# Down projection: nine of 22 pairs with seven products, their weight sums made by accumulating DMAs

## The chip, the cores and the metric

The kernel runs on one core of a Trainium2 chip. TensorE (PE) multiplies, VectorE (DVE) and ScalarE (ACT) do the elementwise work, GpSimd (POOL) and SyncE (SP) can issue DMAs, as ACT can. The metric is the device time of one execution in microseconds; the kernel before took 1520.84 us (median of three runs, 1520.27 to 1521.56).

## The reference

One decoder block on 256 tokens of width 2048, with 16 meta tokens in front. After the attention and recurrence halves (left out here) comes the feed-forward part, whose last product is what the change touches:

```python
def _layer(h, ...):
    ...
    h = h + merged @ w_o
    gate, up = jnp.split(_rms(h, n2) @ w_gu, 2, axis=-1)
    return h + (jax.nn.silu(gate) * up) @ w_dn      # (256 x 5632) @ (5632 x 2048)
```

All tensors are float32.

## The kernel before, in words

A float32 product is made of three matmuls: a number is split into a high part (`float32r`, by an ACT copy) and a low part (DVE: the number minus its high part), and high x high, low x high and high x low are added in PSUM. So each weight block passes through: a load from HBM into a `raw` tile (four buffers, issued by SP), the split into `wh` and `wl` (ACT, then DVE; four buffers each, `WB`), and then the matmuls. The function `product` is one such triple of 512-column matmuls (lines 1460 to 1462).

The down projection contracts over 5632 = 22 pairs of blocks of 128 rows. For each of two column groups `cg` of 1024 columns, a pair is a 2 x 2 block product: two row blocks k of the weight by two column blocks x of 512, against two k by two token halves t of the activations `ach`, `acl`. A plain pair (`slow_jobs`) is two jobs with one 512 KB load and four products each, eight products in all; they add into four PSUM tiles `cs` (named `dn`). A fast pair (`fast_jobs`) makes the same with seven products out of sums of weight blocks and sums of activation blocks (a Winograd form of Strassen's scheme): three of them go to `cs`, four to the PSUM tiles `ps` (named `dnp`), which `sums_of_products` adds and takes apart at the end of a column group. Pairs 0 to 6 are fast.

The sums of activations (`sums_of_pairs`, lines 1431, 1444, 1445) are made once, in batches of pairs, when the up projection ends; they are kept in `sst`, which takes the place of the up projection's input `hts` (the same tag in pool `hp`). The sums of weights are made in each column group: `load2` has four DVE subtractions of 128 x 512 (line 1515) between `raw` tiles and two `tt` tiles, which are then split as weights are.

`run(jobs)` sets the order in which the program is written: it emits the load and split of a job, then the matmuls of the job before (`pending`), so that a load is written one job ahead; `finish_job` emits the last pending matmuls. `slot` counts time in the program's own estimate and emits due streams, such as the batches of `sums_of_pairs`, between products. The engines' final order in this stage is made by a planner that places an instruction on its engine when its inputs and buffers are expected to be there, earlier-written ones first; on the chip each engine and each DMA-issuing queue then runs its own list in order. `ORDER` says which pairs follow each other: in the first column group eight plain pairs, then fast and plain ones in turn; in the second, two plain ones around each fast one, and a plain pair at the end. `post` adds the finished tiles to the residual `hh` and stores it (lines 1561, 1562).

Of the kernel before, what the change touches and what calls it, by code (L numbers as in the profile page):

```python
# [18 lines left out]
P = 128  # L19
# [3 lines left out]
T = 256  # L23
# [18 lines left out]
for _n, _k in (("n1", 16), ("mu", 24), ("mu_w", 1), ("mu_a", 1), ("mu_g", 2), ("w0", 8), ("a0", 8), ("k_k", 8),  # L42
# [22 lines left out]
MIX = 0.47  # L65


FAST = [0, 1, 2, 3, 4, 5, 6]
BATCHES = (2, 2, 2, 1)
SLOW = list(range(7, 22))  # L70
ORDER = [SLOW[:8] + [i for pair in zip(FAST, SLOW[8:]) for i in pair],
         [i for n, f in enumerate(FAST) for i in (SLOW[2 * n], f, SLOW[2 * n + 1])] + SLOW[14:]]
PAIRS = 5500

HOP = 3050
SPREAD = 12000
# [40 lines left out]
def hybrid_block(ctx, tc, A, out, dbg=None):  # L117
# [391 lines left out]
    def split(hi, lo_, src):  # L509
        nc.scalar.activation(hi, src, AF.Copy)  # L510
        nc.vector.tensor_tensor(lo_, src, hi.bitcast(F32), op=ALU.subtract)
# [825 lines left out]
    for j in range(4):  # L1337
        js = slice(j * 512, (j + 1) * 512)
        nc.sync.dma_start(hh[:, :, js], x[:, js].rearrange("(t p) c -> p t c", p=P))

        def post(t, ps, j=j, js=js):
            nc.vector.tensor_tensor(hh[:, t, js], ps, hh[:, t, js], op=ALU.add)
            jk = hp.tile([P, 512], F32, tag="jk", name=f"jk{j}{t}", bufs=2)
            nc.scalar.activation(jk, hh[:, t, js], AF.Square, accum_out=ss2[:, t, j:j + 1])
            if t == 0:
                return
            for k in range(4 * j, 4 * j + 4):
                pt = aux_ps(f"hT{k}")[:, :T]
                for t in range(2):
                    nc.tensor.transpose(pt[:, t * P:(t + 1) * P], hh[:, t, k * P:(k + 1) * P], ident)  # L1350
                tmp = hp.tile([P, T], F32, tag="htmp", name=f"htmp{k}", bufs=3)
# [59 lines left out]
    fast = FAST  # L1411
    slow = [i for i in range(NF // 2) if i not in fast]
    acp_h, acp_l = (t.rearrange("p (i k) (t c) -> p i k t c", k=2, t=2) for t in (ach, acl))
    sst = hp.tile([P, KT, 2, L], F32R, tag="hts", name="sst").rearrange("p k a t -> p (k a t)")
    sst = sst[:, :len(fast) * 6 * P].rearrange("p (i s a c) -> p i s a c", i=len(fast), s=3, a=2)

    def sums_of_pairs():

        at = 0
        for n in BATCHES:  # L1420
            fs, ps_ = slice(at, at + n), slice(fast[at], fast[at] + n)
            at += n
            h = lambda k, t: acp_h[:, ps_, k, t, :].bitcast(F32)
            l = lambda k, t: acp_l[:, ps_, k, t, :].bitcast(F32)
            f = [sst[:, fs, i, 1, :] for i in range(3)] + [acp_l[:, ps_, 0, 1, :]]
            hi = [sst[:, fs, i, 0, :] for i in range(3)] + [acp_h[:, ps_, 0, 1, :]]
            f32 = [hp.tile([P, T], F32, tag="ga", name=f"s{at}{i}", bufs=8)[:, :n * P].rearrange("p (i c) -> p i c", c=P)
                   for i in range(4)]

            def tt(i, x_, y_, op):  # L1430
                nc.vector.tensor_tensor(f32[i], x_, y_, op=op)
# [22 lines left out]
    def rows(ap):  # L1454
        return ap.rearrange("p (r c) -> p r c", c=T)

    def product(ps, a, w, half, first, last):
        o = ps.rearrange("p (a c) -> p a c", a=2)
        hi, lo_ = (x_[:, 2 * half:2 * half + 2] for x_ in w)
        nc.tensor.matmul(o, a[0], hi, start=first, stop=False)  # L1460
        nc.tensor.matmul(o, a[1], hi, start=False, stop=False)  # L1461
        nc.tensor.matmul(o, a[0], lo_, start=False, stop=last)  # L1462
        slot(3 * 512 / 2.4)

    def split_tiles():
        return [wp.tile([P, WCOLS], F32R, tag=t, name=t, bufs=WB).rearrange("p (r c) -> p r c", c=L)[:, :, s:s + T]
                for t, s in zip(("wh", "wl"), PLACE_T)]
# [17 lines left out]
            return load, mul  # L1485
        return [mk(0), mk(1)]

    def fast_jobs(i, cg, cs, ps, end):
        box = {}

        def b(k, x_):
            return wdn[i * 256 + k * P:i * 256 + (k + 1) * P, cg * 1024 + x_ * 512:cg * 1024 + (x_ + 1) * 512]

        def load0():
            ra, rb = (wp.tile([P, 1024], F32, tag="raw", name="raw", bufs=RAWB) for _ in range(2))
            nc.sync.dma_start(ra, wdn[i * 256:i * 256 + P, cg * 1024:(cg + 1) * 1024])
            for x_ in range(2):
                nc.sync.dma_start(rb[:, (1 - x_) * 512:(2 - x_) * 512], b(1, x_))
            box["r"] = rows(ra), rows(rb)
            w = split_tiles()  # L1500
            split(*(t[:, 0:2] for t in w), box["r"][0][:, 0:2])
            return w

        def load1():
            w = split_tiles()
            split(*w, box["r"][1])
            return w

        def load2():
            (b11, b12), (b22, b21) = ([r[:, 0:2], r[:, 2:4]] for r in box["r"])  # L1510
            w, v = split_tiles(), split_tiles()
            ts = [rows(hp.tile([P, 1024], F32, tag="tt", name="tt", bufs=2)) for _ in range(2)]
            t1, t2, t3, t4 = (t[:, 2 * n:2 * n + 2] for t in ts for n in range(2))
            for o, x_, y_ in ((t1, b12, b11), (t2, b22, t1), (t3, b22, b12), (t4, b21, t2)):
                nc.vector.tensor_tensor(o, x_, y_, op=ALU.subtract)
            split(*w, ts[0])
            box["v"] = v, ts[1]
            return w

        def load3():  # L1520
            v, t = box["v"]
            split(*v, t)
            return v

        first = i == fast[0]

        def mul0(w):
            if not ps:
                ps.extend(aux_ps(f"dnp{cg}{n}") for n in range(4))
            product(ps[0], a_of(i, 0, 0), w, 0, first, end)  # L1530

        def mul1(w):
            product(cs[1], s_of(i, 3), w, 0, False, False)
            product(cs[0], a_of(i, 1, 0), w, 1, False, False)

        def mul2(w):
            product(ps[1], s_of(i, 0), w, 0, first, end)
            product(ps[2], s_of(i, 1), w, 1, first, end)

        def mul3(w):  # L1540
            product(ps[3], s_of(i, 2), w, 0, first, end)
            product(cs[2], a_of(i, 1, 1), w, 1, False, False)
            if end:
                sums_of_products(cg, ps)
        return [(load0, mul0), (load1, mul1), (load2, mul2), (load3, mul3)]

    def sums_of_products(cg, ps):
        p1, p5, p6, p7 = ps
        h11, h12, h21, h22 = (hh[:, t, (2 * cg + x_) * 512:(2 * cg + x_ + 1) * 512] for t in range(2) for x_ in range(2))
        u = hp.tile([P, 512], F32, tag="jk", name=f"u{cg}", bufs=2)  # L1550
        nc.scalar.activation(u, p1, AF.Copy)
        for o, x_ in ((u, p6), (h11, p1), (h12, p5), (h12, u), (u, p7), (h22, p5), (h21, u), (h22, u)):
            nc.vector.tensor_tensor(o, x_, o, op=ALU.add)

    def post(cg, t, x_, ps):

# [15 lines left out]
    finish_job()  # L1572
    hp_pool.__exit__(None, None, None)
    ap_pool.__exit__(None, None, None)

# [60 lines left out]
```

## Time and profile before

| what | value |
|---|---|
| median of three runs | 1520.84 us |
| lowest and highest run | 1520.27, 1521.56 us |
| profiled execution: its span, first to last instruction | 1517.7 us; no other time is given for it |
| TensorE busy | 1509.9 us of the span |
| down projection in the trace | 1278.3 us to the end |
| DVE / ACT busy between 1278 and 1514 us | 191.2 / 118.9 us |

The trace names instructions by line, engine and the program's tiles (`wh<-raw` is the high part's split). A matmul's row is longer than the distance to the next one, since matmuls overlap. `L510`/`L511` are the lines of the helper `split` (ACT, DVE), `L335`/`L336` those of the same split inside `wload`, which plain jobs use.

### The profile page before, as it was taken

The numbers are of one execution on the slowest core, as the hardware profiler recorded it, in microseconds if no ns is written. First come the engines' busy times: TensorE is split into PE (matmuls) and PEld (weight loads), VectorE is DVE, ScalarE is ACT, GpSimd is POOL, SyncE is SP. The second block draws the span as 40 slices with busy tenths as digits, with TensorE's granted clock in tenths as the row PEclk, the third lists the DMA queues.
The fourth block names the chain that finished last, engine by engine and source line by source line (L and its number), as shares of the span: only waits on it lengthen the run. The fifth ranks groups of instructions, "written<-read, shape, count | busy, mean of one in ns | idle before, by whom it ended". The sixth has DMA issues, their size and how long they took to land.

```text
span 1517.7 us, 26174 instructions
## 1 busy us (share of the span) xinstructions
PE 1509.9 (99%) x10071; PEld 1339.5 (88%) x10071; DVE 1112.0 (73%) x2009; ACT 808.3 (53%) x1230; POOL 99.3 (7%) x182
## 2 busy tenths in 40 slices
PE   9999999999999999999999999999999999999998
PEld 9999999999989888998888888888888888887887
DVE  7888699689789857875665666566566658879776
ACT  7664565475465545644554555454455545554543
POOL 2112202202202000000000000000000000000000
PEclk9999999999999999999999999999999999999999
DMA  8557456646645757777566666666666666566664
GB/s 271 166 166 212 119 156 185 170 122 173 188 127 149 223 152 214 234 231 240 181 179 192 189 187 193 191 186 192 190 187 191 193 186 182 178 211 201 213 206 138
DMA packets 210365, 283.32 MB, mean 187 GB/s; under 512 B 24320, under 2 KB 129296, under 8 KB 210240
## 3 DMA queue, kind: packets, MB, share of 16 engines
q1 hardware_dynamic: 205344, 277.25, 61.9%
q10 hardware_dynamic: 4896, 4.40, 0.9%
q8 instruction: 79, 1.29, 0.3%
q14 instruction: 46, 0.38, 0.1%
HBM read 274.36 MB, written 7.24 MB: 186 GB/s over the span
## 4 chain that ended last, share of the span: by engine, by line
PE 95%; DVE 3%; DMA 1%; issue 1%; ACT 0%; SPq 0%; DVEq 0%; ACTq 0%
PE up L441 11%; PE gt L441 11%; PE zg L441 8%; PE gt L443 5%; PE up L443 5%; PE dn L1461 4%; PE dn L1460 4%; PE dn L1462 4%; PE zg L443 4%; PE f L441 2%; PE br L365 2%; PE br L366 2%; PE br L367 2%; PE f L365 2%; PE wo L1329 2%; PE wo L1331 2%
## 5 line engine op out<-in xcount | busy, mean ns | idle before, releaser
L336 DVE TENSOR_TENSOR wl<-raw,wh 128x1024 fp32r<-128x1024 f32 x460 | 561.9, 1226 | 281.3 <-ACT wh L335 280.6
L335 ACT ACTIVATE wh<-raw 128x1024 fp32r<-128x1024 f32 x460 | 486.5, 1059 | 470.2 <-PE up L441 118.9
L441 PE MATMUL gt<-hts,wh 128*128 128x512 f32 x704 | 242.9, 393 | 0.0
L441 PE MATMUL up<-hts,wh 128*128 128x512 f32 x704 | 242.7, 392 | 0.0
L443 PE MATMUL gt<-hts,wl 128*128 128x256 f32 x660 | 184.8, 280 | 0.0
L443 PE MATMUL up<-hts,wl 128*128 128x256 f32 x660 | 184.6, 280 | 0.0
L441 PE MATMUL zg<-xhl,wh 128*128 128x512 f32 x512 | 181.2, 399 | 0.0
L441 PEld LDWEIGHTS up<-hts,wh 128*128 128x128 f32 x704 | 130.0, 188 | 25.2
L441 PEld LDWEIGHTS gt<-hts,wh 128*128 128x128 f32 x704 | 129.9, 188 | 25.1
L443 PE MATMUL zg<-xhl,wl 128*128 128x256 f32 x480 | 134.3, 280 | 0.0
L443 PEld LDWEIGHTS up<-hts,wl 128*128 128x128 f32 x660 | 125.3, 190 | 1.8
L443 PEld LDWEIGHTS gt<-hts,wl 128*128 128x128 f32 x660 | 125.3, 190 | 1.8
L441 PEld LDWEIGHTS zg<-xhl,wh 128*128 128x128 f32 x512 | 94.3, 188 | 18.7 <-issue 0.7
L1460 PE MATMUL dn<-wh,ach 128*128 128x512 f32 x282 | 110.7, 393 | 0.0
L1461 PE MATMUL dn<-wh,acl 128*128 128x512 f32 x282 | 110.6, 392 | 0.0
L1462 PE MATMUL dn<-wl,ach 128*128 128x512 f32 x282 | 110.5, 393 | 0.0
L443 PEld LDWEIGHTS zg<-xhl,wl 128*128 128x128 f32 x480 | 90.9, 189 | 1.2
L365 PE MATMUL f<-xhl,wh 128*128 128x272 f32 x256 | 75.9, 296 | 0.0
L367 PE MATMUL f<-xhl,wl 128*128 128x272 f32 x256 | 73.6, 288 | 0.0
L366 PE MATMUL f<-xhl,wh 128*128 128x272 f32 x256 | 73.6, 288 | 0.0
L1462 PEld LDWEIGHTS dn<-wl,ach 128*128 128x128 f32 x282 | 52.9, 187 | 12.3 <-DVE wl L336 0.3
L1461 PEld LDWEIGHTS dn<-wh,acl 128*128 128x128 f32 x282 | 52.9, 188 | 12.0
(493 smaller groups left out, 3056.7 us busy)
## 6 DMA issues: line engine op xcount, KB each, us to landing
raw<-in_w_gate_up_dram SPq DMA_DIRECT2D x176, 512.0 KB, 4.3
raw<-in_w_in_dram SPq DMA_DIRECT2D x160, 512.0 KB, 3.9
raw<-in_w_down_dram SPq DMA_DIRECT2D x74, 512.0 KB, 5.0
raw<-in_w_o_dram SPq DMA_DIRECT2D x32, 512.0 KB, 4.3
raw<-in_w_branch_a_dram SPq DMA_DIRECT2D x16, 512.0 KB, 4.6
raw<-in_w_branch_b_dram SPq DMA_DIRECT2D x16, 512.0 KB, 5.0
raw<-in_w_down_dram SPq DMA_DIRECT2D x28, 256.0 KB, 4.6
zgd<-zg ACTq DMA_DIRECT2D x30, 128.0 KB, 3.8
```

The costliest lines, as they stand in the source:

```text
L335: nc.scalar.activation(th, rr, AF.Copy)
L336: nc.vector.tensor_tensor(tl, rr, th.bitcast(F32), op=ALU.subtract)
L365: nc.tensor.matmul(ps, wh, ah, start=first, stop=False)
L366: nc.tensor.matmul(ps, wh, al, start=False, stop=False)
L367: nc.tensor.matmul(ps, wl, ah, start=False, stop=last)
L441: nc.tensor.matmul(ps.rearrange("p (a t) -> p a t", a=2), wh, act, start=first, stop=last)
L443: nc.tensor.matmul(ps[:, :T], wl, act[:, 0, :], start=False, stop=False)
L1329: nc.tensor.matmul(o, ah[:, kt, ts_], hi, start=first, stop=False)
L1331: nc.tensor.matmul(o, ah[:, kt, ts_], lo_, start=False, stop=last)
L1460: nc.tensor.matmul(o, a[0], hi, start=first, stop=False)
L1461: nc.tensor.matmul(o, a[1], hi, start=False, stop=False)
L1462: nc.tensor.matmul(o, a[0], lo_, start=False, stop=last)
```

## The change

Pairs 0 to 8 are fast, 9 to 21 plain. The weight sums are no longer made by DVE. A fast pair has one kept tile `tt` of 128 x 1024 in each column group (four buffers, `KEPT`). It is loaded with two blocks, split, changed by a DMA that adds blocks from HBM to it (issued by GpSimd), split again, and so on, four steps in all; a block that is wanted alone is loaded over its half by SP. As such a DMA only adds, some sums have their sign turned, and the activation sums and the last additions with them. Each step but the last splits a full tile and makes two products, the last one half a tile and one product. The `raw` tiles serve plain pairs only.

Steps of three fast pairs are taken in turn (`TOGETHER`): first steps of the three, second steps, and so on. Plain jobs are put between them: ten (first column group) or two (second) at the start (`LEAD`), then two after every five or three fast steps (`EVERY`), the last two jobs of a group always plain. First loads of fast pairs are written `FETCH` or more steps ahead. The last up-projection job is finished before the down projection's first load is written, and `sst` and `tt` lie in a new pool `dnp` in the place of `hts`, which has a pool `ht` of its own.

```diff
-FAST = [0, 1, 2, 3, 4, 5, 6]
-BATCHES = (2, 2, 2, 1)
-SLOW = list(range(7, 22))
-ORDER = [...]
+FAST = list(range(9))
+BATCHES = (2, 2, 2, 2, 1)
+SLOW = list(range(9, 22))
+LEAD = (10, 2)
+EVERY = ((2, 5), (2, 3))
+TOGETHER = (3, 3)
 PAIRS = 5500
+FETCH = 4
+KEPT = 4
...
-    hts = hp.tile([P, KT, 2, L], F32R, tag="hts", name="hts")
+    ht_pool = tc.tile_pool(name="ht", bufs=1, reuse_waits="tile")
+    ht = ht_pool.__enter__()
+    hts = ht.tile([P, KT, 2, L], F32R, tag="hts", name="hts")
...
-    sst = hp.tile([P, KT, 2, L], F32R, tag="hts", name="sst").rearrange("p k a t -> p (k a t)")
-    sst = sst[:, :len(fast) * 6 * P].rearrange("p (i s a c) -> p i s a c", i=len(fast), s=3, a=2)
+    finish_job()
+    ht_pool.__exit__(None, None, None)
+    dn_pool = tc.tile_pool(name="dnp", bufs=1, reuse_waits="tile")
+    dn = dn_pool.__enter__()
+    sst = dn.tile([P, len(fast), 3, 2, P], F32R, tag="sst", name="sst")
...
-            tt(0, h(0, 1), h(1, 1), ALU.add)
+            tt(0, h(0, 1), h(1, 1), ALU.subtract)
...
-            tt(0, f32[0], l(1, 1), ALU.add)
+            tt(0, f32[0], l(1, 1), ALU.subtract)
...
-            tt(3, h(1, 0), f32[1], ALU.subtract)
+            tt(3, f32[1], h(1, 0), ALU.add)
...
-        def load0():
-            ra, rb = (wp.tile([P, 1024], F32, tag="raw", name="raw", bufs=RAWB) for _ in range(2))
-            nc.sync.dma_start(ra, wdn[i * 256:i * 256 + P, cg * 1024:(cg + 1) * 1024])
-            for x_ in range(2):
-                nc.sync.dma_start(rb[:, (1 - x_) * 512:(2 - x_) * 512], b(1, x_))
...
-            for o, x_, y_ in ((t1, b12, b11), (t2, b22, t1), (t3, b22, b12), (t4, b21, t2)):
-                nc.vector.tensor_tensor(o, x_, y_, op=ALU.subtract)
...
+        def tile_of():
+            return dn.tile([P, 1024], F32, tag="tt", name="tt", bufs=KEPT)
+
+        def halved(n):
+            t = box["t"]
+            w = split_tiles()
+            split(*(x_[:, :2 * n] for x_ in w), rows(t)[:, :2 * n])
+            return w
+
         def load0():
+            t = box["t"] = tile_of()
+            nc.sync.dma_start(t[:, :512], b(0, 0))
+            nc.sync.dma_start(t[:, 512:], b(1, 1))
+
+        def split0():
+            t = box["t"]
+            w = halved(2)
+            nc.gpsimd.dma_start(t.rearrange("p (x c) -> p x c", x=2),
+                                b(0, 1).unsqueeze(1).to_broadcast([P, 2, 512]), accum_op=ALU.add)
             return w
 
+        def split1():
+            t = box["t"]
+            w = halved(2)
+            nc.gpsimd.dma_start(t[:, :512], b(1, 1), accum_op=ALU.add)
+            nc.sync.dma_start(t[:, 512:], b(1, 0))
             return w
 
+        def split2():
+            t = box["t"]
+            w = halved(2)
+            nc.gpsimd.dma_start(t[:, :512], b(1, 0), accum_op=ALU.add)
             return w
 
+        def split3():
+            return halved(1)
...
         def mul0(w):
             if not ps:
                 ps.extend(aux_ps(f"dnp{cg}{n}") for n in range(4))
             product(ps[0], a_of(i, 0, 0), w, 0, first, end)
+            product(cs[1], s_of(i, 3), w, 1, False, False)
 
         def mul1(w):
-            product(cs[1], s_of(i, 3), w, 0, False, False)
+            product(ps[1], s_of(i, 0), w, 0, first, end)
+            product(ps[3], s_of(i, 2), w, 1, first, end)
+
+        def mul2(w):
+            product(ps[2], s_of(i, 1), w, 0, first, end)
             product(cs[0], a_of(i, 1, 0), w, 1, False, False)
 
-        def mul2(w):
-            product(ps[1], s_of(i, 0), w, 0, first, end)
-            product(ps[2], s_of(i, 1), w, 1, first, end)
-
         def mul3(w):
-            product(ps[3], s_of(i, 2), w, 0, first, end)
-            product(cs[2], a_of(i, 1, 1), w, 1, False, False)
+            product(cs[2], a_of(i, 1, 1), w, 0, False, False)
             if end:
                 sums_of_products(cg, ps)
-        return [(load0, mul0), (load1, mul1), (load2, mul2), (load3, mul3)]
+        return load0, [(split0, mul0), (split1, mul1), (split2, mul2), (split3, mul3)]
...
-        for i in ORDER[cg]:
-            if i in fast:
-                run(fast_jobs(i, cg, cs, ps, i == fast[-1]))
-            else:
-                run(slow_jobs(i, cg, cs, i == ORDER[cg][-1]))
+        plain = [job for i in SLOW for job in slow_jobs(i, cg, cs, i == SLOW[-1])]
+        quick, at = [], 0
+        while at < len(FAST):
+            group = [fast_steps(i, cg, cs, ps, i == FAST[-1]) for i in FAST[at:at + TOGETHER[cg]]]
+            quick += [(load if n == 0 else None, steps[n]) for n in range(4) for load, steps in group]
+            at += TOGETHER[cg]
+        loads = [load for load, _ in quick]
+        lead, (slow_n, quick_n) = LEAD[cg], EVERY[cg]
+
+        def ahead(n):
+            for k in range(n):
+                if loads[k] is not None:
+                    loads[k]()
+                    loads[k] = None
+        run(plain[:lead])
+        del plain[:lead]
+        n = 0
+        while n < len(quick):
+            ahead(min(n + max(FETCH, quick_n), len(quick)))
+            run([step for _, step in quick[n:n + quick_n]])
+            n += quick_n
+            k = min(slow_n, len(plain) - 2)
+            run(plain[:k])
+            del plain[:k]
+        run(plain)
```

More of the change, by code (lines that the diff above doesn't have):

```diff
@@ L65 @@
 MIX = 0.47
-FAST = [0, 1, 2, 3, 4, 5, 6]
-BATCHES = (2, 2, 2, 1)
-SLOW = list(range(7, 22))
-ORDER = [SLOW[:8] + [i for pair in zip(FAST, SLOW[8:]) for i in pair],
-         [i for n, f in enumerate(FAST) for i in (SLOW[2 * n], f, SLOW[2 * n + 1])] + SLOW[14:]]
+FAST = list(range(9))
[4 more added lines that the diff above has]
+TOGETHER = (3, 3)
 PAIRS = 5500
+FETCH = 4
+KEPT = 4
 HOP = 3050
@@ L1350, in post @@
                     nc.tensor.transpose(pt[:, t * P:(t + 1) * P], hh[:, t, k * P:(k + 1) * P], ident)
-                tmp = hp.tile([P, T], F32, tag="htmp", name=f"htmp{k}", bufs=3)
+                tmp = ht.tile([P, T], F32, tag="htmp", name=f"htmp{k}", bufs=3)
                 nc.vector.tensor_scalar(tmp, pt, vc("n2", k), None, op0=ALU.mult)
@@ L1486, in slow_jobs, with fast_steps @@
         return [mk(0), mk(1)]
-    def fast_jobs(i, cg, cs, ps, end):
+    def fast_steps(i, cg, cs, ps, end):
+        first = i == fast[0]
         box = {}
@@ L1492, in b @@
             return wdn[i * 256 + k * P:i * 256 + (k + 1) * P, cg * 1024 + x_ * 512:cg * 1024 + (x_ + 1) * 512]
-        def load0():
-            ra, rb = (wp.tile([P, 1024], F32, tag="raw", name="raw", bufs=RAWB) for _ in range(2))
-            nc.sync.dma_start(ra, wdn[i * 256:i * 256 + P, cg * 1024:(cg + 1) * 1024])
-            for x_ in range(2):
-                nc.sync.dma_start(rb[:, (1 - x_) * 512:(2 - x_) * 512], b(1, x_))
-            box["r"] = rows(ra), rows(rb)
-            w = split_tiles()
-            split(*(t[:, 0:2] for t in w), box["r"][0][:, 0:2])
-            return w
@@ L1504, in load1 @@
-        def load1():
-            w = split_tiles()
-            split(*w, box["r"][1])
-            return w
[L1509 to L1513, printed above, removed]
-            for o, x_, y_ in ((t1, b12, b11), (t2, b22, t1), (t3, b22, b12), (t4, b21, t2)):
-                nc.vector.tensor_tensor(o, x_, y_, op=ALU.subtract)
-            split(*w, ts[0])
-            box["v"] = v, ts[1]
-            return w
@@ L1520, in load3 @@
[L1520 to L1525, printed above, removed]
+        def tile_of():
[5 more added lines that the diff above has]
+            return w
+        def load0():
+            t = box["t"] = tile_of()
+            nc.sync.dma_start(t[:, :512], b(0, 0))
+            nc.sync.dma_start(t[:, 512:], b(1, 1))
@@ L1551, in sums_of_products @@
         nc.scalar.activation(u, p1, AF.Copy)
-        for o, x_ in ((u, p6), (h11, p1), (h12, p5), (h12, u), (u, p7), (h22, p5), (h21, u), (h22, u)):
-            nc.vector.tensor_tensor(o, x_, o, op=ALU.add)
+        for o, x_, op in ((u, p6, ALU.add), (h11, p1, ALU.add), (h12, p5, ALU.add), (h12, u, ALU.subtract),
+                          (u, p7, ALU.add), (h22, p5, ALU.add), (h21, u, ALU.add), (h22, u, ALU.subtract)):
+            nc.vector.tensor_tensor(o, o, x_, op=op)
     def post(cg, t, x_, ps):
```

1 line of the change is left out of this document (added).

## The prediction

> **What bounds the kernel now.** I read the page first, then the busy times of the down-projection stretch, then TensorE's order of time there, then the waits, the groups and the DMA rates.
>
> ```profile
> span 1517.7 us, 26174 instructions
> PE 1509.9 (99%) x10071; PEld 1339.5 (88%) x10071; DVE 1112.0 (73%) x2009; ACT 808.3 (53%) x1230; POOL 99.3 (7%) x182
> ```
>
> TensorE is busy 99% of the span, so only fewer matmuls, or fewer gaps between them, can shorten it. The next fence has the busy times of the stage (columns: PE, weight loads, DVE, ACT, POOL, clock, DMA share, GB/s), then the rows of its two PSUM families, `dn` and `dnp`, in the same stretch.
>
> ```profile
> 1278.00:1514.00 236.00, 235.12 (x1018) 189.96 (x1016) 191.19 (x252) 118.90 (x136) 0.00 (x0) 1.00 0.60 190
> 1278.00:1514.00 236.00, 200.19 (x846) 158.65 (x846) 4.84 (x9) 1.00 0.60 190
> 1278.00:1514.00 236.00, 44.50 (x168) 31.36 (x168) 6.31 (x10) 1.16 (x2) 1.00 0.60 190
> ```
>
> There are 846 + 168 = 1014 matmuls, which is what the code gives: a plain pair is 8 products of 3 matmuls for each of two column groups, a fast pair 7, so 15 x 48 + 7 x 42 = 1014. DVE is busy 81% of the stage, ACT 50%, GpSimd not at all, and the clock is full. The order of time gives the pace and the gaps:
>
> ```profile
> 1278.34 0.40 PE L1460 MATMUL dn<-wh,ach 128*128 128x512 f32 x1
> 1279.72 0.39 PE L1460 MATMUL dn<-wh,ach 128*128 128x512 f32 x1
> ...
> 1378.32 0.39 PE L1461 MATMUL dnp<-wh,sst 128*128 128x512 f32 x1
> 1378.93 0.50 PE L1462 MATMUL dnp<-wl,sst 128*128 128x512 f32 x1 [0.22 <-DVE wl L511]
> ...
> 1403.37 0.39 PE L1462 MATMUL dn<-wl,ach 128*128 128x512 f32 x1
> 1404.31 0.50 PE L1460 MATMUL dnp<-wh,sst 128*128 128x512 f32 x1 [0.55 <-ACT wh L510]
> ...
> 1513.49 0.39 PE L1462 MATMUL dn<-wl,ach 128*128 128x512 f32 x1
> 1513.92 0.76 DVE L1561 TENSOR_TENSOR hh<-dn,hh 128x256 f32<-128x256 f32 x2 [0.62 <-PE dn L1462]
> ```
>
> A matmul's row lasts 0.39 us, but matmuls overlap: the first two rows are six matmuls apart, 1.38 / 6 = 0.23 us each. That is the price of one matmul. All 1013 steps last 1513.49 - 1278.34 = 235.15 us; at 0.23 they would last 233.0, so 2.1 us are gaps. The two quoted are 0.61 - 0.23 = 0.38 and 0.94 - 0.23 = 0.71, together 1.1 us; both end on a split of a fast pair's weights. From the last matmul to the end of the span are 4.0 us of posting.
>
> **The change, part by part.** *Matmuls.* Two pairs more lose one product in each of two column groups: 2 x 2 x 3 = 12 matmuls, 12 x 0.23 = 2.76 us. They lie on the bounding path, with nothing beside them.
>
> *DVE and ACT.* The groups of the stage (count, busy, mean ns, idle before):
>
> ```profile
> L1515 DVE TENSOR_TENSOR tt<-raw,tt 128x512 f32<-128x512 f32 x28 | 19.2, 686 | 11.5 <-DMA raw<-in_w_down_dram 11.4
> L1515 DVE TENSOR_TENSOR tt<-raw 128x512 f32<-128x512 f32 x28 | 19.2, 687 | 12.8 <-DMA raw<-in_w_down_dram 12.6
> L511 DVE TENSOR_TENSOR wl<-tt,wh 128x1024 fp32r<-128x1024 f32 x28 | 34.1, 1222 | 14.4 <-ACT wh L510 14.3
> L510 ACT ACTIVATE wh<-tt 128x1024 fp32r<-128x1024 f32 x28 | 29.6, 1060 | 45.4 <-PE dn L1461 37.9 <-DVE tt L1515 5.8 <-DVE wl L511 1.7
> L1431 DVE TENSOR_TENSOR s<-s,acl 128x256 f32<-128x256 f32 x10 | 3.9, 418 | 0.1
> L1553 DVE TENSOR_TENSOR hh<-dnp,hh 128x512 f32<-128x512 f32 x6 | 3.9, 680 | 0.0
> ```
>
> The 56 subtractions of L1515 leave DVE: 38.4 us. A fast pair keeps three full splits and one half for each column group, a plain pair has two, so two more fast pairs add (3.5 - 2) x 4 = 6 splits: 7.3 us of DVE, 6.4 of ACT. One more batch of two in the activation sums is 14 operations at 0.418, 5.9 us of DVE. DVE falls from 191 to about 166 us, 70% of the stage, and both quoted gaps stood behind splits that followed such subtractions. I count those 1.1 us as regained; the bounds are 0 and the whole 2.1. Turned signs change no count.
>
> *The flush and the new pool at the start.* The last up-projection job is now issued before the first down job's load. If its posting (four `ub` chains of four DVE operations at 0.417 us, 6.7 us) held the first splits, TensorE could wait as long. What hides it is that the instruction order is not the program's: the activation sums, programmed behind the up projection, began long before its end.
>
> ```profile
> L1431 DVE TENSOR_TENSOR s<-ach x8: 281/418/424, 1259.5 to 1305.6; 128x256 f32<-128x256 f32 x6, 128x128 f32<-128x128 f32 x2
> ACT wh L510 <- PE dn L1461: 64.2, 39, 3.1
> L1398 DVE TENSOR_TENSOR ub<-ub,rsb 128x256 f32<-128x256 f32 x4 | 1.5, 417 | 0.0
> ```
>
> The first of these is 19 us before 1278.34, so an operation moves up as soon as its inputs are there. Splits are held by TensorE handing back one of four tile pairs (second row, 39 waits), which puts them some three jobs ahead. Cost 0; with that cover gone, 6.7 us.
>
> *The accumulating DMAs.* This is what the trace of before does not show: GpSimd issues nothing here. Each fast pair and column group gets three, of 512, 256 and 256 KB landed: 54 in all. Each stands between one split and the next split of the same tile, so its time from issue to landing is a wait on the path from step to step. Nearest rows:
>
> ```profile
> raw<-in_w_down_dram SPq DMA_DIRECT2D x57, 512.0 KB, 5.0
> raw<-in_w_down_dram SPq DMA_DIRECT2D x26, 256.0 KB, 4.9
> out_dram<-hh SPq DMA_DIRECT2D x6, 256.0 KB, 2.4
> ```
>
> Below, 2.4 us (a 256 KB DMA with nothing beside it); above, twice a load, 10 us, if the tile is read as slowly as HBM. The load is the nearest row; I take it and add the tile's own bytes at about 400 GB/s (the rates below), 5.0 + 1.3 = 6.3 us for 512 KB and 4.9 + 0.7 = 5.6 for 256. The Trainium skill, "DMA: Bandwidth & Descriptors", section on the anatomy of a DMA on the gpsimd path, gives about 2.0 us plus bytes over 436 GB/s. That would be an estimate of 3.2 us and no wait anywhere; the loads' 5.0 us here, which queue behind one another, are already longer, so I stay with the rows.
>
> What room is there? A split runs 1.06 + 1.22 = 2.3 us. It can begin when TensorE starts the job three before its own, and its successor, three jobs on, must be split before TensorE gets there. A fast step is two products (1.38 us; the last step one, 0.69), a plain job four (2.76). In the first column group plain jobs come two after five fast steps, so six jobs hold at least one: 5 x 1.38 + 2.76 = 9.7, less two splits = 5.1 us. In the second group they come two after three, the successor is five jobs on, and eight jobs are 16.6 us less 4.6 = 12 us. So the second group hides even the 10 us bound. In the first, 6.3 us is 1.2 too long where no plain jobs lie between a step and its successor, at about six places: at most 7 us. As plain jobs whose operands are there move up, I take 0.5 us in all, bounds 0 and 7. If one is late, what queues behind it is ACT's next split and then DVE's, in order; on SP, the plain load of the fourth block and the next tile's loads; and on GpSimd the other accumulations.
>
> *The end.* The eight sums of products (8 x 0.68 = 5.4 us of DVE) now have two plain jobs (5.5 us) behind the last fast step instead of four. All four product tiles are complete one to three steps earlier than before, so they can begin before that step. Cost 0; without that, one split behind them, about 2.5 us late.
>
> Sum on the profiled span: 1517.7 - 2.76 - 1.1 + 0.5 = 1514.3. The median of the three runs, 1520.84, stands 3.1 us above that span; I carry this over: **1517.4 us**.
>
> **The rivals.** *One: the accumulations land late.* It decides from about 5 us, in the first column group only. At 7 us it is 1.9 us at six places, 11 us, of which plain jobs moving up take about half: 1517.4 - 0.5 + 6 = 1523 us, between 1519.5 and 1527. For it: my own 6.3 exceeds 5.1, and the 39 waits of splits for TensorE say that no split is early by more than the four tile pairs allow. Against: the order adapts, as the activation sums show.
>
> *Two: the DMA engines become the bound.* Rates of the whole stage in 40 slices, and of 20 us of it from 1398 in slices of half a microsecond:
>
> ```profile
> GB/s 182 124 253 186 202 151 218 135 159 198 221 135 281 116 286 109 276 122 241 149 274 274 182 257 204 268 172 142 242 160 268 234 114 266 180 162 272 103 0 97
> ...
> GB/s 102 12 197 229 356 381 410 299 217 270 324 295 279 283 328 270 283 279 229 188 94 41 205 352 320 107 131 147 209 156 205 311 381 410 377 320 201 184 98 49
> ```
>
> The stage moved 190 GB/s at share 0.60, so 317 at full share; short bursts reach 410. Bytes rise: a fast pair brings 0.75 MiB plain and 1.0 MiB accumulated for each column group, a plain pair 1.0 MiB. In the first group's mixed stretch (36 fast steps, 43.5 us, and 14 plain jobs, 38.6 us) these are 22.75 MiB (23.9 MB) in 82 us, 290 GB/s: it fits. If an accumulated byte costs two, it is 31.75 MiB (33.3 MB), 406 GB/s: at 380 the stretch takes 88 us, 6 more; at 317, 105, 23 more. So 1523 to 1540, I say 1530. This is the case that ends slower; it decides once an accumulated byte costs between 1.25 (317 GB/s) and 2. The Trainium skill, "Collectives: The Full Stack", section on the bandwidth ceiling, says that a reducing transfer reads two sources on one ring and so runs at half a copy's rate (32.35 against 62.28 GB/s there); no run here shows it yet, and by it this rival is the outcome. Against: the highest rates come in bursts, and the second group has time to spare.
>
> *Three: the end gets longer.* The sums of products hold the last split, 2.5 us, 1519.9.
>
> **Chances.** About 0.2%, 3.0 us, is what a measurement of this kernel can tell from no change: 1517.8 to 1523.9 is "same". Forecast 0.45 (own range 1516.2 to 1519.5: the regained gaps at 2.1, or some of the waits); rival one 0.25, two 0.18, three 0.12. The least time is 1520.84 - 2.76 - 2.1 = 1516.0, so the range begins at 1516.1; it ends at 1529, which leaves out the upper half of rival two and little more. Faster: four fifths of the forecast, 0.37. Slower: nearly half of rival one and nearly all of two, 0.28. Same: the rest, 0.35.
>
> **What would show it.** Right: 1002 matmuls at 0.23 us; no `tt` subtractions on DVE; GpSimd's issues landing in 5 to 7 us; waits of ACT for `tt` that end on a DMA without a gap on TensorE behind them; gaps under 1.5 us in the stage. Rival one: gaps of 1 to 5 us before fast steps in the first column group alone, releaser a DMA into `tt`. Rival two: DMA share above 0.9 there, plain loads landing well above 5 us. Three: a gap before the last two jobs. A gap at the first `dn` matmul would prove the flush mispriced. The forecast is wrong if gaps exceed 4 us.

## The result, and the profile after

The changed kernel takes 1546.39 us (median of four runs, 1545.39 to 1548.36) against 1521.11 us for the kernel before, measured beside it: a ratio of 1.0167, interval 1.0153 to 1.0182. It is slower by 25 us; 1517.4 was predicted, in a range that ended at 1529. The profiled execution has a span of 1545.0 us, 27.3 more than before's. The page begins (span, then busy times of the engines; the last line is the head of its chain of waits):

```profile
span 1545.0 us, 26288 instructions
PE 1520.3 (98%) x10059; PEld 1340.2 (87%) x10059; DVE 1090.8 (71%) x1975; ACT 813.9 (53%) x1242; POOL 155.8 (10%) x236
...
PE 79%; issue 7%; DMA 7%; DVE 5%; ACT 1%; POOL 0%; SPq 0%; DVEq 0%; POOLq 0%; ACTq 0%
```

DVE is busy for less than before (1112.0), as meant. The chain now runs through DMAs for 7% of the span, where before's had 1%. The order of time of TensorE gives the stage's first and last matmul, and two of the gaps, one from each column group:

```profile
1279.01 0.40 PE L444 MATMUL up<-hts,wh 128*128 128x512 f32 x1
1279.24 0.39 PE L1468 MATMUL dn<-wh,ach 128*128 128x512 f32 x1
...
1349.65 0.40 PE L1470 MATMUL dnp<-wl,sst 128*128 128x512 f32 x1
1352.75 0.51 PE L1468 MATMUL dnp<-wh,sst 128*128 128x512 f32 x1 [2.71 <-ACT wh L513]
...
1474.55 0.39 PE L1470 MATMUL dnp<-wl,sst 128*128 128x512 f32 x1
1476.34 0.50 PE L1468 MATMUL dnp<-wh,sst 128*128 128x512 f32 x1 [1.41 <-ACT wh L513]
...
1540.44 0.39 PE L1470 MATMUL dn<-wl,ach 128*128 128x512 f32 x1
```

Worked out as in the prediction: 1540.44 - 1279.24 = 261.2 us for 1001 steps, which at 0.23 would be 230.2. So 31.0 us are gaps, where before had 2.1. That is the whole result: 235.15 became 261.2 (+26.05); the stage began 0.9 later (1279.24 against 1278.34) and 0.35 more lie behind its last matmul, 27.3 together.

Where the gaps lie is read from the busy times by stretch (length; PE, weight loads, DVE, ACT, GpSimd; clock, DMA share, GB/s): the whole stage, the plain jobs at its start, the first column group's mixed stretch, and the second group. The two rows behind them are of the tiles `dn` and `dnp` alone.

```profile
1279.00:1541.00 262.00, 244.38 (x1005) 190.47 (x1003) 170.59 (x218) 124.77 (x148) 53.33 (x54) 0.97 0.89 226
1281.00:1314.00 33.00, 32.63 (x143) 26.26 (x142) 30.25 (x59) 19.17 (x31) 5.00 (x5) 1.00 0.89 241
1314.00:1411.00 97.00, 83.53 (x323) 62.15 (x322) 57.56 (x73) 43.63 (x52) 21.71 (x23) 0.95 0.91 217
1411.00:1536.00 125.00, 121.39 (x514) 96.83 (x513) 78.02 (x77) 60.42 (x63) 26.62 (x27) 0.99 0.91 234
...
1279.00:1541.00 262.00, 193.59 (x786) 150.29 (x786) 4.83 (x9) 0.97 0.89 226
...
1279.00:1541.00 262.00, 63.63 (x216) 40.59 (x216) 6.73 (x10) 1.16 (x2) 0.97 0.89 226
```

786 + 216 = 1002 matmuls, twelve fewer, as forecast. A stretch's length less its matmuls at 0.23 us is what it lost: 0.1 us in the plain stretch, 97 - 74.3 = 22.7 in the first group, 125 - 118.2 = 6.8 in the second. The same subtraction is used for every experiment below. The DMA share rose from 0.60 to 0.89, though the rate rose only from 190 to 226 GB/s.

The waits of the stage (total us, times, longest) say on what the splits waited:

```profile
ACT wh L513 <- DMA tt<-in_w_down_dram: 78.7, 37, 7.9
DVE wl L514 <- ACT wh L513: 77.5, 47, 7.3
...
PE dnp L1468 <- ACT wh L513: 9.3, 7, 2.7
...
PE dn L1468 <- ACT wh L513: 2.2, 1, 2.2
```

ACT waited 37 times for a DMA into a kept tile, and DVE's half of the split stood behind ACT's (47 times). Most of these waits cost nothing, since the split was still early enough. TensorE itself waited for the high part of a fast split at eight places, six of them in the first group (from 1325.79 to 1388.36) and two in the second. The DMA view of the stage (packets, MB and share of the 16 engines for each queue; then KB each and median us to landing) has the cause:

```profile
q1 hardware_dynamic: 21664, 40.54, 46.2%
q0 software_dynamic: 10080, 18.88, 41.6%
...
raw<-in_w_down_dram SPq DMA_DIRECT2D x46, 512.0 KB, 6.7
tt<-in_w_down_dram SPq DMA_DIRECT2D x54, 256.0 KB, 6.3
tt<-in_w_down_dram POOLq DMA_DIRECT2D x18, 512.0 KB, 9.5
tt<-in_w_down_dram POOLq DMA_DIRECT2D x36, 256.0 KB, 6.0
```

Queue q0 is GpSimd's and holds nothing but the accumulations. 18.88 MB take 41.6% of the engines' time there, 2.20% for each MB; the loads on q1 take 46.2 / 40.54 = 1.14%. An accumulated byte costs 1.93 times a loaded one. The Trainium skill, "Collectives: The Full Stack", section "The bandwidth ceiling", says that a reducing transfer reads two sources and so runs at half a copy's rate; its two figures, 62.28 and 32.35 GB/s for collective transfers, also stand at 1.93 to 1, and this trace agrees with the ratio. That the two reads are the reason is not shown here.

A 512 KB accumulation lands after 9.5 us, where I had priced 6.3. The order of time shows why the last of three is later still. These are GpSimd's issues of one step's three accumulations (one for each tile of the group), and then ACT's splits that wait for them:

```profile
1335.93 1.20 POOL L1522 DMA_DIRECT2D tt<-in_w_down_dram  x1 [7.73 <-DVE wl L514]
...
1340.79 1.21 POOL L1522 DMA_DIRECT2D tt<-in_w_down_dram  x1 [0.92 <-DVE wl L514]
```

```profile
1343.51 1.06 ACT L513 ACTIVATE wh<-tt 128x1024 fp32r<-128x1024 f32 x1 [2.46 <-DMA tt<-in_w_down_dram]
1346.47 1.06 ACT L513 ACTIVATE wh<-tt 128x1024 fp32r<-128x1024 f32 x1 [1.90 <-DMA tt<-in_w_down_dram]
1351.64 1.06 ACT L513 ACTIVATE wh<-tt 128x1024 fp32r<-128x1024 f32 x1 [4.11 <-DMA tt<-in_w_down_dram]
```

The splits start 7.6, 7.8 and 10.9 us behind their issues. The packets that the trace records for q0 (us from the span's start) give the reason:

```
accumulation   issued    first packet   last packet ends
first          1335.93   1337.86        1341.70
second         1338.64   1341.54        1346.00
third          1340.79   1346.01        1350.66
```

The second begins when the first has ended, and the third when the second has: one queue, one after another, 3.8 to 4.7 us each. TensorE's gap from 1349.65 to 1352.75 is the third of these.

In the second group all three places with gaps have the same origin, the third accumulation of a level: 512 KB each, issued at 1423.73, 1462.21 and 1502.96; their splits start at 1436.05, 1475.23 and 1514.43, just ahead of the gaps that end at 1437.16, 1476.34 and 1516.80. In the first group the queue is not the whole story. TensorE's wait that ends at 1384.33 is for the first accumulation of a level, issued at 1372.95: nothing was left in its queue since 1369.17, and the DMA share was 0.34 to 0.58 from 1374 to 1377, yet its first packet came at 1377.14. The third accumulation ahead of the gap at 1325.79 also began 2.1 us after the queue was free. Why these two began late is open. With what follows them, the two places make some 10 of the first group's 22.7 us.

### The profile page after: what moved, and what is told of

It reads as the page before. It is cut to its first block, busy times and chain, and to the rows that moved or that the text cites. A ratio compares the mean times of both kernels' runs of the same rounds, so it can differ in the third digit from the quotient of the medians.

```text
span 1545.0 us, 26288 instructions
## 1 busy us (share of the span) xinstructions
PE 1520.3 (98%) x10059; PEld 1340.2 (87%) x10059; DVE 1090.8 (71%) x1975; ACT 813.9 (53%) x1242; POOL 155.8 (10%) x236
## 3 DMA queue, kind: packets, MB, share of 16 engines
q0 software_dynamic: 10080, 18.88, 7.2%
## 4 chain that ended last, share of the span: by engine, by line
PE 79%; issue 7%; DMA 7%; DVE 5%; ACT 1%; POOL 0%; SPq 0%; DVEq 0%; POOLq 0%; ACTq 0%
PE gt L444 10%; PE up L444 10%; PE zg L444 8%; DMA tt<-in_w_down_dram 6%; PE gt L446 5%; PE up L446 5%; PE zg L446 4%; PE f L444 2%; PE br L368 2%; PE br L369 2%; PE br L370 2%; PE f L368 2%; PE wo L1334 2%; PE wo L1336 2%; PE wo L1335 2%
## 5 line engine op out<-in xcount | busy, mean ns | idle before, releaser
L339 DVE TENSOR_TENSOR wl<-raw,wh 128x1024 fp32r<-128x1024 f32 x452 | 552.3, 1225 | 294.7 <-ACT wh L338 293.5
L338 ACT ACTIVATE wh<-raw 128x1024 fp32r<-128x1024 f32 x452 | 476.7, 1058 | 474.8 <-PE up L444 121.7
L514 DVE TENSOR_TENSOR wl<-tt,wh 128x1024 fp32r<-128x1024 f32 (+1 forms) x72 | 78.0, 1090 | 77.5 <-ACT wh L513 77.5
L513 ACT ACTIVATE wh<-tt 128x1024 fp32r<-128x1024 f32 (+1 forms) x72 | 67.9, 950 | 103.5 <-DMA tt<-in_w_down_dram 78.7
L1468 PE MATMUL dn<-wh,ach 128*128 128x512 f32 x262 | 104.9, 400 | 2.2 <-ACT wh L513 2.2
L1522 POOL DMA_DIRECT2D tt<-in_w_down_dram x18 | 22.0, 1237 | 835.5 <-DVE wl L514 822.2
L1470 PE MATMUL dn<-wl,ach 128*128 128x512 f32 x262 | 104.9, 400 | 0.8 <-DVE wl L339 0.8
L1469 PE MATMUL dn<-wh,acl 128*128 128x512 f32 x262 | 104.1, 397 | 0.0
```

Of the source, the lines that this page charges most:

```text
L338: nc.scalar.activation(th, rr, AF.Copy)
L339: nc.vector.tensor_tensor(tl, rr, th.bitcast(F32), op=ALU.subtract)
```

## The experiments

I held two theories. *Engines*: the 16 engines are full, since an accumulated byte costs two, and everything on them is late. *Path*, later called *queue*: a level (the same step of a group's three tiles) has three accumulations that follow each other in one queue, about 12 us for three of 512 KB and 8 us for three of 256 KB (from first to last packet, the changed kernel's levels take 10.2 to 12.8 and 6.3 to 10.1 us); TensorE's work of a level is three fast steps, 4.1 us, plus the plain jobs among them, 3.3 us at two in five (7.4), 5.5 us at two in three (9.7), 8.3 us at three in three (12.4). What is missing is a gap.

**Plain writes in place of accumulations.**

```diff
-                                b(0, 1).unsqueeze(1).to_broadcast([P, 2, 512]), accum_op=ALU.add)
+                                b(0, 1).unsqueeze(1).to_broadcast([P, 2, 512]))
...
-            nc.gpsimd.dma_start(t[:, :512], b(1, 1), accum_op=ALU.add)
+            nc.gpsimd.dma_start(t[:, :512], b(1, 1))
...
-            nc.gpsimd.dma_start(t[:, :512], b(1, 0), accum_op=ALU.add)
+            nc.gpsimd.dma_start(t[:, :512], b(1, 0))
```

> The changed kernel with GpSimd's 54 DMAs writing over the tile in place of adding to it, so the weight sums are left out and the products are of single blocks; bytes from HBM, issues, waits and order stay. Theory of the full engines (an accumulated byte costs the DMA engines about two: 41.6% of their time for 18.88 MB against 46.2% for 40.54 MB): their queue's share falls to about 20%, the stage's DMA share from 0.88 to about 0.70, gaps on TensorE to under 8 us, time 1519 to 1526 us. Theory of the path (the distance between a split and its successor is too short for any DMA issued by GpSimd): gaps stay above 15 us, time 1533 us or more.

Measured: 1527.32 us, ratio 1.0044 (1.0028 to 1.0060), between the two expectations. The stage's queues, and the mixed stretches of the two groups:

```profile
q1 hardware_dynamic: 21113, 39.47, 50.2%
q0 software_dynamic: 5472, 18.88, 24.7%
```

```profile
1314.00:1408.00 94.00, 88.13 (x364) 67.79 (x363) 63.95 (x79) 46.66 (x55) 13.75 (x23) 0.98 0.78 254
1408.00:1510.00 102.00, 102.00 (x443) 82.89 (x442) 65.77 (x61) 54.19 (x56) 15.59 (x26) 1.00 0.78 253
```

With the same bytes, queue and waits, q0 costs 1.31% for each MB against 1.27% on q1, both of this kernel's shorter stage: the double cost is the accumulation's, not the queue's. The gaps fall to 10.3 us in the first group and 0.1 in the second. So the accumulation's extra cost made 19 of the 29.5 us. Some 10 are left in the first group, where DMAs at about a load's price still come too late; what makes them was not isolated.

**Half the first accumulation.** Only one half of the tile is added to in the first step; with fewer bytes in q0 the waits stay.

```diff
-            nc.gpsimd.dma_start(t.rearrange("p (x c) -> p x c", x=2),
-                                b(0, 1).unsqueeze(1).to_broadcast([P, 2, 512]), accum_op=ALU.add)
+            nc.gpsimd.dma_start(t[:, :512], b(0, 1), accum_op=ALU.add)
```

> The changed kernel with the first accumulation of each fast pair going to one half of the tile (256 KB) and not to both, so that the sum in the other half is left out. Theory of the queue (a level's three accumulations run one after another, 4 us each for 512 KB and 2.7 for 256): the first level needs 8 us as the others do, so the second column group, whose gaps all stand between first and second steps, loses under 1.5 us in place of 6.7, the first some 12 to 17 in place of 23: 1530 to 1537 us. Theory that only the stage's DMA share counts (0.88 goes to some 0.81): gaps shrink everywhere alike, a quarter of 30 us, 1539 us.

Measured: 1530.90 us, ratio 1.0069 (1.0051 to 1.0087).

```profile
1314.00:1411.00 97.00, 88.82 (x351) 67.65 (x350) 62.33 (x76) 45.33 (x54) 19.27 (x23) 0.95 0.87 228
1411.00:1523.00 112.00, 112.00 (x486) 90.97 (x485) 72.39 (x70) 58.36 (x60) 23.29 (x27) 1.00 0.84 213
```

The second group loses nothing (486 x 0.23 = 111.8 of 112), the first 16.3. For the second group this is what the queue gives: all three levels now need about 8 us, under its 9.7, and its loss was the 512 KB level alone, as the order of time of the changed kernel has it too. For the first group only the direction fits. Levels of 8 us against 7.4 would lose 0.6 us each, some 5 us for nine, so two thirds of the 16.3 are not explained by this sum.

**Six pairs, three plain jobs to three fast steps.** The same form, with sums that are complete, and the room that the queue asks for.

```diff
-FAST = list(range(9))
-BATCHES = (2, 2, 2, 2, 1)
-SLOW = list(range(9, 22))
-LEAD = (10, 2)
-EVERY = ((2, 5), (2, 3))
+FAST = list(range(6))
+BATCHES = (2, 2, 2)
+SLOW = list(range(6, 22))
+LEAD = (6, 6)
+EVERY = ((3, 3), (3, 3))
...
-PAIRS = 5500
+PAIRS = 2500
```

> The accumulating form with six fast pairs in two groups of three and three plain jobs after every three steps in both column groups (12.4 us of work for a level), the sums made and used. Theory of the queue: a level's three accumulations then fit, gaps under 3 us; one pair fewer than before costs 1.4 us: 1522 to 1525 us. If the engines' total time binds whatever the spacing, over 1530 us.

Measured: 1521.10 us, ratio 1.0007 (0.9996 to 1.0017). Stretches of the two groups, and ACT's wait for the kept tiles:

```profile
1281.00:1396.00 115.00, 114.88 (x498) 93.19 (x497) 81.14 (x104) 59.22 (x69) 17.91 (x18) 1.00 0.91 254
1398.00:1511.00 113.00, 113.00 (x491) 91.95 (x491) 66.03 (x62) 52.36 (x53) 17.71 (x18) 1.00 0.78 208
```

```profile
ACT wh L513 <- DMA tt<-in_w_down_dram: 16.8, 8, 3.1
```

No gap is left (114.5 of 115, 112.9 of 113), at the same DMA share, 0.91, at which the changed kernel lost 22.7 us. So the share alone does not decide; with room for a level nothing is lost. The form itself is free where 12.4 us of work stand beside a level. Nine pairs cannot have that: 36 fast steps for a column group would want 36 plain jobs, and 13 plain pairs give 26.

**All plain jobs spread at two in three, and the same with plain writes.**

```diff
-LEAD = (10, 2)
-EVERY = ((2, 5), (2, 3))
+LEAD = (2, 2)
+EVERY = ((2, 3), (2, 3))
...
-PAIRS = 5500
+PAIRS = 1000
```

> The changed kernel with the first column group spaced as the second (two plain jobs at the start, then two after every three fast steps), the activation sums written earlier for it. In the changed kernel the first group had 23 us of gaps and slow clock, the second 6.7. Theory of the queue (three accumulations of a level run one after another, some 12 us for the 512 KB ones and 8 for the others, against 7.4 us of work for a level at two plain jobs in five steps and 9.7 at two in three): the first group's loss falls to the second's, 13 us in all, time 1530 us, between 1527 and 1534. Theory that the first group loses for another reason (late activation sums, the flush): it stays above 15 us there, 1540 us or more.

> The kernel before this one with GpSimd's DMAs writing over the tile in place of adding, the weight sums left out. With plain writes in the old spacing the second group had no gap at all and the first 10.4 us; with both groups spaced wide and plain writes the two causes (an accumulated byte's double cost, too narrow a first group) are both gone: gaps under 2 us, time 1517 to 1519 us, the 2.76 us of saved matmuls showing. If a third cause is left, 1521 us or more.

Measured: 1554.16 us (1.0221, 1.0199 to 1.0242) with accumulations, 1532.37 (1.0078, 1.0061 to 1.0095) with plain writes, both far above what was expected. The stretches, of the first kernel and then of the second:

```profile
1284.00:1322.00 38.00, 24.77 (x85) 17.43 (x84) 27.07 (x55) 17.55 (x27) 6.43 (x6) 0.88 0.64 154
1322.00:1420.00 98.00, 93.06 (x388) 73.63 (x387) 62.74 (x72) 48.61 (x54) 20.26 (x21) 0.98 0.94 243
1420.00:1541.00 121.00, 115.87 (x490) 92.29 (x489) 73.08 (x71) 57.22 (x60) 26.61 (x27) 0.99 0.90 229
```

```profile
1284.00:1320.00 36.00, 26.65 (x93) 18.51 (x92) 29.57 (x64) 19.70 (x30) 4.59 (x7) 0.91 0.60 183
1322.00:1420.00 98.00, 98.00 (x426) 79.54 (x425) 67.56 (x68) 51.62 (x54) 13.58 (x22) 1.00 0.83 279
1420.00:1520.00 100.00, 100.00 (x435) 81.22 (x434) 64.91 (x63) 53.21 (x55) 14.15 (x24) 1.00 0.72 234
```

Both lose much in their first stretch (18.5 and 14.6), where the fast steps now come right at the start: in the first kernel, up to 1322, ACT waits 16.5 us for DMAs into kept tiles, and DVE's share of the activation sums waits 10.0 us for ACT. That part is my edit's and says nothing of the queue. Behind it the accumulating kernel loses 8.8 and 8.3 us, the other nothing (98.0 of 98, 100.1 of 100). At two in three a level of three plain writes fits into 9.7 us and a level of three 512 KB accumulations does not, in either column group.

**Accumulations that nobody waits for, and the form with seven pairs.** Both were meant to separate the theories and did not.

```diff
...
+    def aside():
+        turn[0] += 1
+        return sc[turn[0] % 2]
...
-            nc.gpsimd.dma_start(t.rearrange("p (x c) -> p x c", x=2),
+            nc.gpsimd.dma_start(aside().rearrange("p (x c) -> p x c", x=2),
...
```

> The accumulating form with seven fast pairs, its 42 accumulations going to two scratch tiles that nothing reads, so that no split waits for them and the weight sums are left out; to be read beside the next kernel, which is the same with the sums. Theory of the full engines: the loads still land late, time within 6 us of the next kernel's, 1533 us or more. Theory of the path: the gaps go although the DMA share stays where it is, time 1519 to 1525 us.

> The changed kernel with seven fast pairs in place of nine, as before, and all else of the change. If the accumulating form is the loss and grows with the number of accumulations, 42/54 of the 28 us of gaps stay, 22 us, and no matmul is saved: 1540 us, between 1535 and 1546. If two pairs too many are the loss, 1520 to 1526 us.

Measured: 1549.63 us (1.0191, 1.0169 to 1.0212) and 1566.53 us (1.0302, 1.0281 to 1.0322), the second 20 us above the end of its expected range. Seven pairs in groups of three leave a last group of one, whose steps stand close behind each other, each waiting for its own accumulation. In the kernel with seven pairs one such wait of TensorE, ending at 1390.59, lasts 4.22 us.

The accumulations that were set aside wait for one another, since two scratch tiles take turns, and plain loads came late too (waits of that kernel's stage):

```profile
POOL sc L1538 <- DMA sc<-in_w_down_dram: 54.3, 14, 9.7
...
ACT wh L338 <- DMA raw<-in_w_down_dram: 33.1, 12, 8.6
```

So ACT waited 33.1 us for plain loads: what the engines theory says can happen, in a kernel that has two other faults. It isn't evidence for either.

**Nine pairs by DVE, as before did seven; and the start alone.** The first takes the kernel before with nine pairs and an order with room for them; the second takes it with the flush and the new pool of the change.

```diff
-FAST = [0, 1, 2, 3, 4, 5, 6]
-BATCHES = (2, 2, 2, 1)
-SLOW = list(range(7, 22))
+FAST = list(range(9))
+BATCHES = (2, 2, 2, 2, 1)
+SLOW = list(range(9, 22))
-ORDER = [...]
+ORDER = [...]
```

```diff
...
+    finish_job()
+    ht_pool.__exit__(None, None, None)
+    dn_pool = tc.tile_pool(name="dnp", bufs=1, reuse_waits="tile")
+    dn = dn_pool.__enter__()
...
```

> The kernel before with nine fast pairs in its own form (weight sums by DVE), plain and fast pairs in turn. The count alone: 12 matmuls fewer, 2.76 us; if DVE, at 81% of the stage before and some 24 us of work more, still hides it, 1518.3 us; if it doesn't, gaps before fast steps and 1521 to 1526 us.

> The kernel before with the flush of the last up-projection job and the new pool alone. My step priced it at 0: 1521 us within 1. If the flush held the first splits: up to 6.7 us more and a gap at the first matmul of the down projection.

Measured: nine pairs by DVE 1521.91 us, ratio 1.0012 (1.0003 to 1.0022); the start alone 1521.23 us, 1.0003 (0.9994 to 1.0013). The start costs nothing. The two stretches of nine pairs by DVE:

```profile
1281.00:1396.00 115.00, 112.18 (x484) 90.11 (x483) 108.58 (x167) 65.13 (x82) 0.00 (x0) 1.00 0.58 184
1398.00:1511.00 113.00, 111.47 (x477) 88.35 (x476) 95.05 (x109) 57.69 (x60) 0.00 (x0) 1.00 0.62 197
```

They lose 3.7 and 3.3 us, more than the 2.76 that twelve matmuls save; DVE is busy for 94% of the first (108.58 of 115). ACT's splits wait 26.9 us for DVE's subtractions (5.8 before), and TensorE's longest wait, 1.83 us, ends on DVE's half of a split. So DVE was a limit for nine pairs in this order, and the change had a real one to remove; another order was not tried.

**Six pairs by DVE and three by accumulation, set wide apart.** The version to which the runs pointed: pairs 0 to 2 keep their tile and accumulate, one pair at a time, and pairs 3 to 8 use before's subtractions on DVE, so that both queues have room.

```diff
+KEEP = (0, 1, 2)
+FROM = (11, 2)
+STEP_OF = (3, 4)
-KEPT = 4
+KEPT = 3
...
```

> Nine fast pairs, six of them with weight sums by DVE as before (with turned signs), three with a kept tile and accumulating DMAs, whose twelve steps stand one after every three (first column group) or four jobs (second) of the others, so a level has 20 us or more. Theory of the queue: 18 accumulations with that room cost nothing; DVE has 48 subtractions in place of 56 and some 199 us of 236; gaps at most those before, 1.7 us: 1002 matmuls save 2.76 us, 1517 to 1518.5 us. If nine pairs lose their gain to something else than the accumulations, as nine by DVE alone did (7 us of gaps), 1520 to 1523 us.

Measured: 1522.41 us (eleven runs, 1520.24 to 1524.66), ratio 1.0012 (1.0003 to 1.0021): no gain.

```profile
1310.00:1395.00 85.00, 81.27 (x350) 65.04 (x349) 75.42 (x104) 48.93 (x59) 7.59 (x8) 1.00 0.77 216
1396.00:1511.00 115.00, 115.00 (x501) 93.48 (x500) 89.05 (x98) 59.41 (x61) 8.84 (x9) 1.00 0.71 204
```

Its second group is without gaps (501 x 0.23 = 115.2). The first loses 4.5 us, and most of it is one place: TensorE waits for DVE's half of a split, and ahead of that split DVE stood idle for an ordinary load, which it needs for a subtraction.

```profile
1332.11 0.69 DVE L1585 TENSOR_TENSOR tt<-raw 128x512 f32<-128x512 f32 x1 [3.16 <-DMA raw<-in_w_down_dram]
...
1333.99 0.50 PE L1469 MATMUL dnp<-wl,sst 128*128 128x512 f32 x1 [3.13 <-DVE wl L513]
```

That load, 512 KB issued at 1323.81, landed after 8.2 us (median before: 5.0). Beside it ran an accumulation issued at 1322.24, which landed after 10.3 us, and the DMA share from 1329 to 1332.2 was 1.01, that is, full. So here a load came late on full engines beside a single accumulation: what the engines theory says, in a place where no level of three stood in the queue. This profiled execution is one of its fastest runs (1520.42); what the slower ones lose more was not looked into. No kernel tried beats the one before.

## Why the prediction was wrong

*What held.* Twelve matmuls fewer at 0.23 us. DVE at 170.6 us in the stage, 166 predicted. The flush at the start: the first `dn` matmul follows the last `up` by 0.23 us (1279.01, 1279.24), and the start alone measures as before. The end: no gap in front of the last two jobs, so rival three falls. That before's gaps of 2.1 us came from DVE fits the six pairs, which have no subtractions and no gaps, but that was not isolated.

*The step that failed* is "I take 0.5 us in all, bounds 0 and 7" for the accumulations' waits, which cost 29.5 us in the two groups' mixed stretches, slow clock behind the waits included. Three things were wrong in it. First, the price of one: "6.3 us for 512 KB" was a load plus the tile's own bytes at the copy rate; 9.5 were measured, close to the 10 us that I had as the bound. For 256 KB it was nearly right, 5.6 against 6.0. Second, and worth more, I set each accumulation against the time between a step and its own successor: 5.1 us in the first group, and "12 us", so "the second group hides even the 10 us bound". I never put the three accumulations of a level behind one another, although I had read that the loads' 5.0 us include such queueing. A 512 KB level needs 12.8 us (first packet 1337.86 to last 1350.66) where 7.4 or 9.7 us of work stand beside it. The second group's 6.8 us, and their absence at half the bytes and with plain writes, show that step's failure best. Third, what a late one costs: "at about six places" was right for the first group, but they and one wait for a plain job's split took 22.7 us, over 3 us a place, where 1.2 had been set.

The rooms were counted wrongly as well, with less effect. Where a step's successor is three jobs on, the six jobs hold two plain ones, not one: 11.0 - 4.6 = 6.4 us, which would have hidden 6.3. In the second group the third step of a level has three plain jobs among its eight, 15.2 - 4.6 = 10.6 us and not 12. Its third 512 KB accumulations were the late ones there: their splits start 12.3, 13.0 and 11.5 us behind the issues.

*Rival one* had the place and the releaser right (a gap before a fast step, a split that waits for a DMA into `tt`), but said the first column group only, and 6 us where 22.7 were lost.

*Rival two* had the cause, an accumulated byte that costs two, and said 1530, at most 1540. Its own upper estimate for the first group's mixed stretch, 23 us more at 317 GB/s, is what was lost there (22.7). That it came out so near is luck: the engines are not simply full, since the six pairs ran without a gap at the same share, 0.91. Its signs were there, a share above 0.9 and plain loads that landed after 6.7 us in the median (12.2 between 1425 and 1520) against 5.0 before, but ACT waited for plain loads for only 2.1 us in the whole stage. I left the second group out of it, "has time to spare"; and I wrote that by the Trainium skill's rule on a reducing transfer this rival was the outcome, and still gave it 0.18. The double cost and the queue act together: the accumulation's double price lengthens each turn in the queue. How much a second queue for accumulations would give back was not tried.

*The clock* was in no case. Of the gaps, 27 steps at 0.43 us (27 x 0.20 = 5.4 us) are not waits at all but matmuls at a lower granted clock, behind two waits in a row; see the last section.

## What to carry to other kernels

When transfers of one kind share a queue, price a level of them, not one: add up the turns of all that are issued together and set the sum against the work that lies between two levels. An accumulating DMA took the engine time of 1.93 loaded bytes for each byte here, so moving additions from DVE to DMA pays only where the DMA engines have that room and each level has work enough beside it. A change that saves 2.76 us on a full engine is best tried where it leaves every other margin alone; here each way to the two extra pairs cost more than that in gaps.

## What the hardware showed that I had not expected

The granted clock falls after short gaps. The stretch from 1327 to 1332 us (clock: the third number from the end), and the order of time in it:

```profile
1327.00:1332.00 5.00, 4.95 (x15) 3.91 (x16) 4.48 (x9) 2.59 (x4) 0.85 (x1) 0.66 0.63 145
```

```profile
1325.79 0.50 PE L1468 MATMUL dnp<-wh,sst 128*128 128x512 f32 x1 [1.46 <-ACT wh L513]
...
1327.05 0.50 PE L1470 MATMUL dnp<-wl,sst 128*128 128x512 f32 x1 [0.53 <-DVE wl L514]
...
1328.17 0.63 PE L1468 MATMUL dn<-wh,ach 128*128 128x512 f32 x1
1328.60 0.63 PE L1469 MATMUL dn<-wh,acl 128*128 128x512 f32 x1
```

Two waits of 1.46 and 0.53 us, with two matmuls between them, are soon followed by steps of 0.43 us in place of 0.23, from 1328.17 to 1331.16: 3.0 us. The Trainium skill, "TensorE: Matmul & The Clock Gate", Part 1, puts the halved clock behind at least one idle window of about 3.4 us. The length of the slow stretch is near that, but the trace does not agree on the cause: no such window was idle, and two waits of 2.0 us together were enough. The longer wait quoted above, 2.71 us at 1352.75, was followed by no such steps, so what decides it is open. A late DMA thus costs its wait here and, at times, about 1.4 us more (7 steps at 0.20).

The second surprise stands in the packets above: the three accumulations of a level hardly overlapped at all, although all three had been issued before the first one's packets had ended.
